# Output projection's second half begun in the score banks, beside the last head's values

## The chip, the cores and the metric

The kernel runs on one core of a Trainium2 chip, as one program. The metric is device time in microseconds (us), the median of several runs. The core's engines are TensorE (PE, its weight loads shown apart as PEld), VectorE (DVE), ScalarE (ACT), GpSimd (POOL) and SyncE (SP, which issues DMAs). Matmuls write to PSUM, which has 8 banks of 512 fp32 columns on 128 partitions; the other engines read it from there.

## The reference

One layer of a streaming encoder: RMSNorm and one input projection, two groups of eight attention heads (latent attention, group A, heads 0 to 7; forgetting attention, group B, heads 8 to 15), one output projection over both groups, and a SwiGLU FFN. It is computed for a new stream of 1040 rows and for 32 rows that continue a cache of 512. Cut to what matters here:

```python
D_MODEL = 1024; D_FF = 2816
mixed = jnp.concatenate([o_a.reshape(B, L, 512), o_b.reshape(B, L, 512)], axis=-1)

def finish_layer(x, mixed, w_out, norm_ffn, w_gate, w_up, w_down):
    x = x + mixed @ w_out
    h = rms_norm(x, norm_ffn)
    return x + (jax.nn.silu(h @ w_gate) * (h @ w_up)) @ w_down

y = rms_norm(x, norm_final)
```

## The kernel before

All 1072 rows (32 and 1040) are columns of transposed tiles. A product in fp32 accuracy is made of three matmuls: each operand is split into a high and a low part (`hi`, `lo`), and hi x hi, hi x lo and lo x hi are added in PSUM. The program has four stages: the projections; attention over heads 8 to 15 and then 0 to 7 (0 to about 689 us with the first stage); the second half of the output projection with the FFN's norm (to about 752); the FFN in 22 blocks of 128 hidden rows and the final norm (to the end).

**Attention.** `attention` walks over the heads. For each it makes the scores (`scores`, into a pair of PSUM banks, tag psS, two pairs), and beside the scores of one set of tiles it steps through the values of the set before (`values`, and after each second head `finish_pair`; the generator `state["pend"]`): transposes into psT, value matmuls into po, ScalarE and VectorE move the results. Between, it steps through a `filler`, other work for TensorE: for heads 0 to 7 this is `out_half`, the output projection's first half (the rows of `w_out` that belong to group B, accumulated in psF, 48 steps, written to DRAM as `sX2`). How often a filler step is taken is `rate`: steps / (25 (heads - 0.7)). At the start of the last head what is left of the filler is drained. After the last head's scores nothing is left to run beside its values and the last `finish_pair`: `for _ in state["pend"]: pass`.

**PSUM.** In attention psS holds 4 banks, psT 2, psO 1 and psF 1. All close with `B.close()`. The stage after opens psG with six single banks and psN with two.

**Output projection, second half.** Eight row blocks m, each with three column chunks (`FC`: 408, 408 and 256 columns), make 24 units. A unit sums k = 0 to 3 with three matmuls each. Units go in groups of four: k = 0, 1, 2 of the four units first, then k = 3 of the four; k = 3 stands for the last pair of heads. VectorE then adds the unit to `x2`, which has been loaded from `sX2`.

**FFN.** For each block f and chunk, `gate_up` makes two products of 24 matmuls (gate, up), which VectorE reads with L877 and L882, and `down` makes, for the block before, eight products of three matmuls, each read by VectorE with L898 (added to `x2`). The weights of the block after are split by ScalarE (`gh`, `dh`) and VectorE (`gl`, `dl`, L68). The last block's third chunk ends in `down_final`, which keeps eight products in four banks.

The order of instructions on each engine is made by a scheduler in the framework from the program and its tiles; each engine then works through its own queue. A tile framework puts the semaphores: an instruction that writes a tile waits for what read or wrote that tile before. Names in the rows are tiles; L12 is line 12.

Of the kernel before, what the change touches and what calls it, by code (L numbers as in the profile page):

```python
# [9 lines left out]
F32 = mybir.dt.float32  # L10
# [39 lines left out]
def trunk(ctx: ExitStack, tc: tile.TileContext, a):  # L50
# [53 lines left out]
    def rows4(t):  # L104
        return t.rearrange("p (k t) -> p k t", k=4)
# [330 lines left out]
    tp = B.enter_context(tc.tile_pool(name="tp", bufs=LAG + 1))  # L436
    st = B.enter_context(tc.tile_pool(name="st", bufs=2))

    psS = B.enter_context(tc.tile_pool(name="psS", bufs=2, space=PSUM))
    psT = B.enter_context(tc.tile_pool(name="psT", bufs=2, space=PSUM))  # L440
    psO = B.enter_context(tc.tile_pool(name="psO", bufs=1, space=PSUM))
    psF = B.enter_context(tc.tile_pool(name="psF", bufs=1, space=PSUM))
# [280 lines left out]
    state = {"pend": iter(()), "n": 0}  # L723

    def attention(hs, filler, steps, last):
        rate, owed = steps / (25.0 * (len(hs) - 0.7)), [0.0]

        def fill():
            if last and h == hs[0] and grps[0][0] == 5:
                return  # L730
            owed[0] += rate
            while owed[0] >= 1:
                next(filler, None)
                owed[0] -= 1

        rs = raw = None
        for h in hs:
            nxt = h + 1 if h + 1 < 16 else 0
            if not (last and h == hs[-1]):
                heads[nxt] = 0  # L740
            ops, v = heads.pop(h)
            if h == hs[-1]:
                for _ in filler:
                    pass
                if not last:
                    masks()
            nops = fetch(nxt) if nxt in heads else None
            if h % 2 == 0:
                rs = st.tile([128, 2, 9], F32, tag="rs", name="rs")
                pool.memset(rs, 1.0)  # L750
                raw = st.tile([128, T], F32, tag="raw", name="raw", bufs=1)
            for grps in (((5, 6, 7, 8),), ((1, 2, 3, 4), (0,))):
                todo = [i for g in grps for i in g]
                P, done = {}, 0
                for j, i in enumerate(todo):
                    P[i] = scores(h, ops, i, rs)
                    fill()
                    while done < (j + 1) * state["n"] // len(todo):
                        next(state["pend"], None)
                        fill()  # L760
                        done += 1
                for _ in state["pend"]:
                    pass
                if nops is not None and len(grps) == 1:
                    heads[nxt] = (nops, fetch_v(nxt))
                gens = [values(h, v, [(i, P[i]) for i in g], raw) for g in grps]
                state["n"] = sum(len(g) + g[0] if g != (0,) else 1 for g in grps)
                if h % 2 == 1 and len(grps) == 2:
                    gens.append(finish_pair(h // 2, rs, raw))
                    state["n"] += 3  # L770
                state["pend"] = chain(*gens)
        for _ in filler:
            pass
# [6 lines left out]
    def masks():  # L780
        B3 = rooms[-1][:106]
        for j, part in enumerate((0, 0, 1)):
            move(B3[32 * j:32 * j + 32], sKR[:, part])
        move(B3[96:106], sMK[0:10])
        mixed["B3"] = B3
# [2 lines left out]
    mixed["A"] = (slot("A_hi"), slot("A_lo"))  # L788

    attention(range(0, 8), out_half(), 48, True)  # L790
    for _ in state["pend"]:
        pass
    B.close()
    hpx.close()
# [2 lines left out]
    with ExitStack() as C:  # L797
# [1 line left out]
        sqp = C.enter_context(tc.tile_pool(name="sqpC", bufs=1, side="right"))  # L799
        ap_ = C.enter_context(tc.tile_pool(name="ap", bufs=2, side="right"))  # L800
        wf = C.enter_context(tc.tile_pool(name="wpf", bufs=2))
        psG = C.enter_context(tc.tile_pool(name="psG", bufs=6, space=PSUM))
        psN = C.enter_context(tc.tile_pool(name="psNF", bufs=2, space=PSUM))

        def ffn_weights(f):
            gh = wf.tile([128, 2, 8, 128], FR, tag="gh", name="gh")
# [23 lines left out]
                marks[1] = eng.tensor_tensor(out=acc[:, cs], in0=acc[:, cs], in1=sq[:, :n], op=ALU.add).ins  # L830

        big = [tuple(rows4(t) for t in mixed[g]) for g in ("A", "B")]
        m_hi, m_lo = big[0]
        W = None
        units = [(m, c) for m in range(8) for c in FC]
        for u0 in range(0, len(units), 4):
            part = []
            for m, (c0, n) in units[u0:u0 + 4]:
                out_weights(8 + m + 2)
                part.append((m, c0, n, psG.tile([128, 512], F32, tag="psG", name="psG"), w_ring[8 + m]))  # L840

            for ks in ((0, 1, 2), (3,)):
                for m, c0, n, ps, w in part:
                    for k in ks:
                        pe.matmul(ps[:, :n], w[0][:, k], m_hi[:, k, c0:c0 + n], start=(k == 0), stop=False)
                        pe.matmul(ps[:, :n], w[0][:, k], m_lo[:, k, c0:c0 + n], start=False, stop=False)
                        pe.matmul(ps[:, :n], w[1][:, k], m_hi[:, k, c0:c0 + n], start=False, stop=(k == 3))
            if u0 == 12:
                W = ffn_weights(0)
            for m, c0, n, ps, w in part:  # L850
                cs = slice(c0, c0 + n)
                dve.tensor_tensor(out=x2[:, m, cs], in0=ps[:, :n], in1=x2[:, m, cs], op=ALU.add)
                square(m, cs, n, dve)
                if m == 7:

                    for k in range(8):
                        hi, lo = (t[:, k % 4, cs] for t in big[k // 4])
                        act.activation(hi, x2[:, k, cs], AF.Copy, scale=g_ffn[:, k:k + 1])
                        dve.scalar_tensor_tensor(lo, x2[:, k, cs], g_ffn[:, k:k + 1], f32(hi), ALU.mult, ALU.subtract)
                    ps = psN.tile([128, 512], F32, tag="psn", name="psn")  # L860
                    pe.matmul(ps[:, :n], ones, acc[:, cs], start=True, stop=True)
                    rsqrt(rb[:, cs], ps, n, D, sqp)


        def gate_up(W, c0, n, ah, al, between=None):
# [1 line left out]
            cs = slice(c0, c0 + n)  # L867

            def product(j):
                ps = psG.tile([128, 512], F32, tag="psG", name="psG")  # L870
                marks[2] = mm3(ps[:, :n], lambda k: gh[:, j, k], lambda k: gl[:, j, k], lambda k: big[k // 4][0][:, k % 4, cs], lambda k: big[k // 4][1][:, k % 4, cs], 8)
                return ps

# [19 lines left out]
        def down(parts, c0, n, norm=False, then=None):  # L893
            cs = slice(c0, c0 + n)
            for m in range(8):
                ps = psG.tile([128, 512], F32, tag="psG", name="psD")
                down_mm(ps[:, :n], m, cs, parts, True, True)
                dve.tensor_tensor(out=x2[:, m, cs], in0=ps[:, :n], in1=x2[:, m, cs], op=ALU.add)  # L898
                if norm:
                    square(m, cs, n, pool if m < 6 else dve)  # L900
                if m == 3 and then is not None:
                    norm_table()
                    final(*then)
# [19 lines left out]
        def down_final(prev, cur, c0, n):  # L923

            cs = slice(c0, c0 + n)
            pairs = [psG.tile([128, 512], F32, tag="psG", name="psD").rearrange("p (a b) -> p a b", a=2) for _ in range(4)]
            for part in (prev, cur):

                with tc.issue_after(marks[2]):
# [159 lines left out]
```

## Time and profile before

| | us |
|---|---|
| median of 3 runs | 1536.96 (1535.45 to 1539.69) |
| the profiled execution | 1537.25 |
| its span | 1535.5 |
| TensorE busy | 1493.0 |
| VectorE busy | 971.5 |
| ScalarE busy | 591.4 |
| mean granted TensorE clock | 0.993 |

The time is read from TensorE: it works all but some 42 us of the span. The page's slices of the span show where it doesn't (in the attention part and at the end), the windows show this per stretch, and the timelines name for an idle time the instruction that ended it. A matmul's row lasts longer than the distance to the next one's start, since they are pipelined; the pitch is read from starts. [...]

### The profile page before, as it was taken

Reading aid. Unit: us, or ns where it says so; the run is one execution under the profiler, and the core shown is the slowest. Engines: PE = TensorE matmul, PEld = TensorE weight load, DVE = VectorE, ACT = ScalarE, POOL = GpSimd, SP = SyncE. Lnnn points to the kernel's source line nnn. Section 1 sums busy time; section 2 is a strip of 40 time slices with the busy share of each in tenths; the row PEclk is TensorE's granted clock in tenths of the full one; section 3 lists DMA queues with packets and bytes.
Section 4 is the critical chain, followed back from the end, with each engine's and each line's share of the span. In section 5 each row is a group of like instructions: output and inputs, shape, how many; then the busy total and the mean of one; then the engine's idle time right before and its main releaser. Section 6 shows DMA issues by size and latency. Waiting matters only on the chain.

```text
span 1535.5 us, 24295 instructions
## 1 busy us (share of the span) xinstructions
PE 1493.0 (97%) x9317; PEld 1433.5 (93%) x9317; DVE 971.5 (63%) x1861; ACT 591.4 (39%) x1198; POOL 198.5 (13%) x331
## 2 busy tenths in 40 slices
PE   9999998999898999989999999999999999999996
PEld 8999997888787898979999999999999999999996
DVE  8874626787966776766855655555555555655547
ACT  7443436777655666654511111111111121111124
POOL 0343242422131211200000000000000000000001
PEclk9999999999999999999999999999999999999999
DMA  6689567778587686515111111111111111111003
GB/s 196 233 258 299 172 210 249 238 218 262 147 238 185 174 212 161 148 41 206 34 50 44 54 42 42 42 42 42 42 42 42 53 58 53 44 42 42 28 1 115
DMA packets 87636, 184.19 MB, mean 120 GB/s; under 512 B 9754, under 2 KB 52954, under 8 KB 87428
## 3 DMA queue, kind: packets, MB, share of 16 engines
q1 hardware_dynamic: 70592, 128.34, 28.8%
q0 software_dynamic: 16928, 54.29, 10.1%
q8 instruction: 74, 1.21, 0.3%
q14 instruction: 42, 0.34, 0.1%
HBM read 123.93 MB, written 58.67 MB: 119 GB/s over the span
## 4 chain that ended last, share of the span: by engine, by line
PE 88%; DVE 4%; ACT 3%; issue 2%; DMA 1%; POOL 1%; DVEq 0%; SPq 0%; POOLq 0%; ACTq 0%
PE psG L122 11%; PE psG L121 11%; PE psG L123 11%; PE psD L890 5%; PE psD L891 5%; PE psD L889 5%; PE psS L589 5%; PE psT L651 4%; PE psA L123 3%; PE psA L121 3%; PE psA L122 3%; PE po L667 2%; PE po L668 2%; PE psA L386 1%; PE psA L387 1%
## 5 line engine op out<-in xcount | busy, mean ns | idle before, releaser
L898 DVE TENSOR_TENSOR x<-psD,x 128x408 f32<-128x408 f32 (+1 forms) x496 | 236.2, 522 | 4.3 <-PE psD L891 4.3
L122 PE MATMUL psG<-B_lo,gh 128*128 128x408 f32 (+1 forms) x528 | 172.8, 327 | 0.0
L121 PE MATMUL psG<-B_hi,gh 128*128 128x408 f32 (+1 forms) x528 | 172.8, 327 | 0.0
L122 PE MATMUL psG<-A_lo,gh 128*128 128x408 f32 (+1 forms) x528 | 172.6, 327 | 0.0
L121 PE MATMUL psG<-A_hi,gh 128*128 128x408 f32 (+1 forms) x528 | 172.3, 326 | 0.0
L891 PE MATMUL psD<-ah,dl 128*128 128x408 f32 (+1 forms) x528 | 172.1, 326 | 0.0
L123 PE MATMUL psG<-B_hi,gl 128*128 128x408 f32 (+1 forms) x528 | 171.8, 325 | 0.0
L123 PE MATMUL psG<-A_hi,gl 128*128 128x408 f32 (+1 forms) x528 | 171.8, 325 | 0.0
L890 PE MATMUL psD<-al,dh 128*128 128x408 f32 (+1 forms) x528 | 171.7, 325 | 0.0
L889 PE MATMUL psD<-ah,dh 128*128 128x408 f32 (+1 forms) x528 | 170.9, 325 | 0.5 <-ACT ah L67 0.5
L878 ACT ACTIVATE sl<-sl 128x408 f32<-128x408 f32 (+1 forms) x66 | 33.1, 503 | 351.3 <-DVE sl L877 351.2
L882 DVE TENSOR_TENSOR sq<-psG,rb 128x408 f32<-128x408 f32 (+1 forms) x66 | 35.0, 530 | 156.5 <-PE psG L123 156.5
L68 DVE TENSOR_TENSOR ptl<-psT,pth 128x512 fp32r<-128x512 f32 x192 | 104.6, 552 | 28.7 <-ACT pth L67 26.6
L592 DVE TENSOR_REDUCE nm<-psS 128x1 f32<-128x656 f32 (+2 forms) x144 | 104.0, 724 | 27.2 <-PE psS L589 25.6
L67 ACT ACTIVATE pth<-psT 128x512 fp32r<-128x512 f32 (+4 forms) x208 | 99.2, 480 | 55.7 <-PE psT L651 46.5
L830 POOL TENSOR_TENSOR acc<-acc,sq 128x408 f32<-128x408 f32 x10 | 10.8, 1076 | 812.4 <-ACT sq L829 811.9
L877 DVE TENSOR_TENSOR sl<-psG,rb 128x408 f32<-128x408 f32 (+1 forms) x66 | 34.9, 530 | 123.0 <-PE psG L123 123.0
L67 ACT ACTIVATE ah<-sl 128x408 fp32r<-128x408 f32 (+1 forms) x66 | 33.2, 503 | 197.2 <-DVE sl L883 125.8
L589 PE MATMUL psS<-b,a 128*128 128x328 f32 (+4 forms) x360 | 99.9, 331 | 7.4 <-ACT pb L597 6.1
L889 PEld LDWEIGHTS psD<-ah,dh 128*128 128x128 f32 x528 | 99.2, 188 | 0.9 <-ACT ah L67 0.7
L122 PEld LDWEIGHTS psG<-B_lo,gh 128*128 128x128 f32 x528 | 99.2, 188 | 0.5 <-issue 0.3
L121 PEld LDWEIGHTS psG<-B_hi,gh 128*128 128x128 f32 x528 | 99.2, 188 | 0.5 <-issue 0.2
(274 smaller groups left out, 3803.5 us busy)
## 6 DMA issues: line engine op xcount, KB each, us to landing
sg<-w_gu SPq DMA_DIRECT2D x44, 512.0 KB
a<-sQ SPq DMA_DIRECT2D x56, 268.0 KB
b<-sK SPq DMA_DIRECT2D x32, 396.0 KB
sg<-w_down SPq DMA_DIRECT2D x22, 512.0 KB
v<-sV SPq DMA_DIRECT2D x16, 512.0 KB
wst<-w_in SPq DMA_DIRECT2D x13, 512.0 KB
sV<-vt POOLq DMA_DIRECT2D x24, 256.0 KB, 4.5
sK<-room POOLq DMA_DIRECT2D x14, 396.0 KB, 4.9
```

The lines of the kernel that those rows point to most:

```text
L67: first = act.activation(hi, src, AF.Copy)
L68: return first.ins, eng.tensor_tensor(out=lo, in0=src, in1=f32(hi), op=ALU.subtract).ins
L121: pe.matmul(ps, whi(k), rhi(k), start=(k == 0), stop=False)
L122: pe.matmul(ps, whi(k), rlo(k), start=False, stop=False)
L123: last = pe.matmul(ps, wlo(k), rhi(k), start=False, stop=(k == K - 1))
L589: pe.matmul(out, qa[:K, t0:t0 + nq], kb[:K, k0 + c:k0 + c + w], start=(j == 0), stop=last)
L592: dve.tensor_reduce(out=nm[:nq, j:j + 1], in_=src, axis=AX.XY if len(src.shape) == 3 else AX.X, op=ALU.max, negate=True)
L651: pe.transpose(out=pt[:, 128 * g:128 * g + 128], in_=tiles[g][1][:, c:c + 128], identity=ident)
L889: pe.matmul(ps, dh[:, m], ah[:, cs], start=first and j == 0, stop=False)
L890: pe.matmul(ps, dh[:, m], al[:, cs], start=False, stop=False)
L891: pe.matmul(ps, dl[:, m], ah[:, cs], start=False, stop=last and j == len(parts) - 1)
L898: dve.tensor_tensor(out=x2[:, m, cs], in0=ps[:, :n], in1=x2[:, m, cs], op=ALU.add)
```

## The change

The pool psS stays open to the end. During the last head the filler isn't drained ahead, and its rate divides by heads - 0.25. Beside the nine steps of the last head's values and `finish_pair`, `begin` draws two psS pairs and fills their four halves with k = 0, 1, 2 of the first four units, one k per step. The first group then has only k = 3 to do. After that six banks go around: the four halves (`early`) and two banks of psG (was six). `bank` deals them out in that order to units, gate/up products and down products alike.

```diff
-    psS = B.enter_context(tc.tile_pool(name="psS", bufs=2, space=PSUM))
+    psS = ctx.enter_context(tc.tile_pool(name="psS", bufs=2, space=PSUM))
...
-        rate, owed = steps / (25.0 * (len(hs) - 0.7)), [0.0]
+        rate, owed = steps / (25.0 * (len(hs) - (0.25 if last else 0.7))), [0.0]
...
-            if h == hs[-1]:
+            if h == hs[-1] and not last:
                 for _ in filler:
                     pass
-                if not last:
-                    masks()
+                masks()
...
+    units = [(m, c) for m in range(8) for c in FC]
+
+    def out_products(unit, ps, ks):
+        (m, (c0, n)), w = unit, w_ring[8 + unit[0]]
+        for k in ks:
+            for j, (wj, t) in enumerate(((0, 0), (0, 1), (1, 0))):
+                pe.matmul(ps[:, :n], w[wj][:, k], rows4(mixed["A"][t])[:, k, c0:c0 + n], start=(k == 0 and j == 0), stop=(k == 3 and j == 2))
+
+    early = []
+
+    def begin():
+        for u in (0, 2):
+            out_weights(10)
+            pair = psS.tile([128, 2, 512], F32, tag="psS", name="psS")
+            for j in range(2):
+                early.append(pair[:, j])
+                for k in range(3):
+                    out_products(units[u + j], pair[:, j], (k,))
+                    yield
+
+    begun = begin()
     for _ in state["pend"]:
+        next(begun, None)
+    for _ in begun:
         pass
     B.close()
...
-        psG = C.enter_context(tc.tile_pool(name="psG", bufs=6, space=PSUM))
+        psG = C.enter_context(tc.tile_pool(name="psG", bufs=2, space=PSUM))
...
+        drawn = [4]
+
+        def bank():
+
+            t = drawn[0] % 6
+            drawn[0] += 1
+            return early[t] if t < 4 else psG.tile([128, 512], F32, tag="psG", name="psG")
...
-                part.append((m, c0, n, psG.tile([128, 512], F32, tag="psG", name="psG"), w_ring[8 + m]))
...
+                part.append((m, c0, n, early[len(part)] if u0 == 0 else bank(), w_ring[8 + m]))
+
+            for ks in ((3,),) if u0 == 0 else ((0, 1, 2), (3,)):
+                for j, (m, c0, n, ps, w) in enumerate(part):
+                    out_products(units[u0 + j], ps, ks)
...
             def product(j):
-                ps = psG.tile([128, 512], F32, tag="psG", name="psG")
+                ps = bank()
...
             for m in range(8):
-                ps = psG.tile([128, 512], F32, tag="psG", name="psD")
+                ps = bank()
...
-            pairs = [psG.tile([128, 512], F32, tag="psG", name="psD").rearrange("p (a b) -> p a b", a=2) for _ in range(4)]
+            pairs = [bank().rearrange("p (a b) -> p a b", a=2) for _ in range(4)]
```

The rows below are queue order, with the tile numbers behind the names and the engines on whose semaphores an instruction waits. In the changed kernel psS_8425 and psS_8513 are the two pairs; a row does not say which half it writes, so the text does. L797, L915 to L917 and L924 of the changed kernel are the lines 845 to 847, 889 to 891 and 898 of before; L903 and L908 are 877 and 882.

On TensorE, at the last head's values, before: the last transposes and values (L706, L637) stand alone, and the projection's first matmul (L845) waits behind them.

```order
L706 MATMUL psT_8488<-ident_62,bc_8474 128x128 x3
L665 MATMUL po_8438<-ptm_2591,v_7937 128x512
L706 MATMUL psT_8500<-ident_62,bc_8482 128x128 [waits DVE_49,Pool_49]
L637 MATMUL po_8502<-pth_8464,v_7937 128x96 [waits DMAHW0_49,DVE_49]
L637 MATMUL po_8502<-pth_8464,v_7937 128x96 x4
L845 MATMUL psG_8558<-A_hi_5600,woh_8066 128x408 [waits DVE_49,PE_49]
```

The same engine in the changed kernel, from the first of the early products (L797) on.

```order
L668 MATMUL po_8285<-ptl_8378,v_7913 128x128
L797 MATMUL psS_8425<-A_hi_5600,woh_8168 128x408
L797 MATMUL psS_8425<-A_lo_5601,woh_8168 128x408
L797 MATMUL psS_8425<-A_hi_5600,wol_8169 128x408
L651 MATMUL psT_8429<-ident_62,pa_8249 128x128 [waits DVE_49]
L651 MATMUL psT_8429<-ident_62,pa_8296 128x128
L651 MATMUL psT_8429<-ident_62,pa_8326 128x128
L665 MATMUL po_8285<-ptm_2591,v_7913 128x512 [waits DMAHW4_49,DMAHW3_49,Pool_49]
L797 MATMUL psS_8425<-A_hi_5600,woh_8168 128x408
```

Three early matmuls each now stand between the steps of the last values.

On TensorE, at the end of an FFN block before: the last two down products of the 256-column chunk, then the next block's first gate/up product (L121). Each takes the next of six banks.

```order
L889 MATMUL psD_11144<-ah_10546,dh_10220 128x256 [waits DVE_49]
L890 MATMUL psD_11144<-al_10547,dh_10220 128x256
L891 MATMUL psD_11144<-ah_10546,dl_10221 128x256
L889 MATMUL psD_11149<-ah_10546,dh_10220 128x256 [waits DVE_49]
L890 MATMUL psD_11149<-al_10547,dh_10220 128x256
L891 MATMUL psD_11149<-ah_10546,dl_10221 128x256
L121 MATMUL psG_11174<-A_hi_5600,gh_10842 128x408 [waits DVE_49]
```

The same place in the changed kernel.

```order
L915 MATMUL psS_8425<-ah_10447,dh_10141 128x256 [waits DVE_49]
L916 MATMUL psS_8425<-al_10448,dh_10141 128x256
L917 MATMUL psS_8425<-ah_10447,dl_10142 128x256
L915 MATMUL psS_8513<-ah_10447,dh_10141 128x256 [waits DVE_49]
L916 MATMUL psS_8513<-al_10448,dh_10141 128x256
L917 MATMUL psS_8513<-ah_10447,dl_10142 128x256
L121 MATMUL psS_8425<-A_hi_5600,gh_10723 128x408 [waits DVE_49]
```

The down products here write the second halves of the two pairs; L121 writes the first half of psS_8425, and the read that its wait names is VectorE's read of the second half, three matmuls back. In the same chunk, ahead of that, between the two gate/up products of the changed kernel:

```order
L123 MATMUL psS_8513<-B_hi_2593,gl_10432 128x256
L915 MATMUL psG_10979<-ah_10447,dh_10141 128x256 [waits Activation_49]
L916 MATMUL psG_10979<-al_10448,dh_10141 128x256
L917 MATMUL psG_10979<-ah_10447,dl_10142 128x256
L915 MATMUL psG_10984<-ah_10447,dh_10141 128x256
L916 MATMUL psG_10984<-al_10448,dh_10141 128x256
L121 MATMUL psS_8513<-A_hi_5600,gh_10431 128x256 [waits DVE_49]
```

L123 ends the first product in one half of psS_8513, L121 begins the second in the other half, five matmuls later; its wait names VectorE's read of the first half (L903). Before, the second product followed the first at once, in another bank.

On VectorE, where the FFN begins, before: the first read of a gate product (L877) follows L110 at once.

```order
L859 SCALAR_TENSOR_TENSOR B_lo_2594<-x2_8541,gains_61,B_hi_2593 128x256 [waits Activation_49]
L110 TENSOR_SCALAR rv_9082<-psn_9080 128x256 [waits DVE_49,PE_49]
L877 TENSOR_TENSOR sl_9108<-psG_9110,rb_8542 128x408
L882 TENSOR_TENSOR sq_9109<-psG_9137,rb_8542 128x408
L114 TENSOR_TENSOR rv_9082<-rv_9082,rr_9084 128x256 [waits DVE_49,Activation_49]
```

In the changed kernel that read is L903.

```order
L110 TENSOR_SCALAR rv_9067<-psn_9065 128x256 [waits DVE_49,PE_49]
L68 TENSOR_TENSOR gl_9076<-sg_9083,gh_9075 128x1024 [waits DMAHW7_49]
L114 TENSOR_TENSOR rv_9067<-rv_9067,rr_9069 128x256 [waits DVE_49,Activation_49]
L68 TENSOR_TENSOR dl_9078<-sg_9087,dh_9077 128x1024 [waits DMAHW0_49]
L115 TENSOR_TENSOR rv_9067<-rv_9067,rr_9069 128x256 [waits DVE_49]
L903 TENSOR_TENSOR sl_9093<-psS_8425,rb_8585 128x408
```

Two weight splits (L68) and two small steps now stand between.

## Rows read from the trace of the kernel before

In the windows the engines' busy times stand in the order PE, PEld, DVE, ACT, POOL, each with its number of instructions. In the timelines the first number is the start, the second how long it took.

**Rows 1.** Page, part 1: engines' busy time, share of span, instructions.

```profile
PE 1493.0 (97%) x9317; PEld 1433.5 (93%) x9317; DVE 971.5 (63%) x1861; ACT 591.4 (39%) x1198; POOL 198.5 (13%) x331
```

**Rows 2.** Windows, last head: stretch, length, engines' busy us, clock, DMA share, GB/s.

```profile
655.00:670.00 15.00, 13.46 (x86) 11.67 (x86) 10.45 (x20) 9.19 (x23) 1.08 (x2) 1.00 0.13 43
...
677.00:685.00 8.00, 6.00 (x40) 4.61 (x38) 5.22 (x11) 4.41 (x10) 1.83 (x6) 1.00 0.01 2
685.00:687.00 2.00, 0.90 (x5) 0.60 (x4) 1.36 (x3) 1.11 (x2) 0.01 (x1) 0.93 0.02 4
687.00:688.80 1.80, 0.71 (x4) 0.57 (x4) 1.54 (x6) 0.83 (x3) 0.00 (x0) 0.50 0.06 19
688.80:693.40 4.60, 4.59 (x14) 4.48 (x15) 0.58 (x2) 0.14 (x1) 0.00 (x0) 0.50 0.98 368
```

**Rows 3.** Timeline, TensorE, last head: start, us, operation, idle before and releaser.

```profile
680.83 0.50 PE L667 MATMUL po<-pth,v 128*128 128x512 f32 x1 [0.42 <-DVE raw L678]
681.16 0.39 PE L668 MATMUL po<-ptl,v 128*128 128x512 f32 x1
681.40 0.34 PE L667 MATMUL po<-pth,v 128*128 128x384 f32 x1
...
686.53 1.18 PE L637 MATMUL po<-pth,v 112*128 112x96 f32 x5 [0.90 <-DVE raw L678]
688.81 0.68 PE L845 MATMUL psG<-A_hi,woh 128*128 128x408 f32 x1 [1.10 <-DVE raw L712]
```

**Rows 4.** Timeline, TensorE's weight loads, last head.

```profile
680.83 0.19 PEld L667 LDWEIGHTS po<-pth,v 128*128 128x128 f32 x1 [0.61 <-DVE raw L678]
```

**Rows 5.** Timeline, VectorE, last head.

```profile
680.09 0.69 DVE L678 TENSOR_TENSOR raw<-po,half 64x512 f32<-64x512 f32 x1
...
688.46 0.20 DVE L712 TENSOR_TENSOR raw<-raw,psT 128x48 f32<-128x48 f32 x1
```

**Rows 6.** Timeline, SyncE's queue, where the projection's second half begins.

```profile
687.74 3.92 SPq L58 DMA_DIRECT2D x<-sX  x8
```

**Rows 7.** Windows, one stretch of the FFN (columns as in Rows 2).

```profile
1004.00:1040.00 36.00, 36.00 (x223) 35.93 (x222) 20.05 (x40) 6.20 (x9) 0.00 (x0) 1.00 0.14 45
```

**Rows 8.** Timeline, TensorE, one FFN block: 256-column chunk, then 408.

```profile
1005.44 0.28 PE L123 MATMUL psG<-B_hi,gl 128*128 128x256 f32 x1
...
1008.29 0.28 PE L123 MATMUL psG<-B_hi,gl 128*128 128x256 f32 x1
...
1011.24 0.35 PE L121 MATMUL psG<-A_hi,gh 128*128 128x408 f32 x1
...
1015.53 0.35 PE L123 MATMUL psG<-B_hi,gl 128*128 128x408 f32 x1
```

**Rows 9.** Timeline, VectorE, same FFN block.

```profile
1005.76 0.42 DVE L877 TENSOR_TENSOR sl<-psG,rb 128x256 f32<-128x256 f32 x1 [1.75 <-PE psG L123]
...
1015.91 0.58 DVE L877 TENSOR_TENSOR sl<-psG,rb 128x408 f32<-128x408 f32 x1 [0.81 <-PE psG L123]
```

**Rows 10.** Timelines at the FFN's start: TensorE, then VectorE.

```profile
738.20 0.36 PE L121 MATMUL psG<-A_hi,gh 128*128 128x408 f32 x1
...
740.05 0.88 PE L861 MATMUL psn<-acc,ones 128*128 128x408 f32 x2
...
740.96 0.35 PE L123 MATMUL psG<-A_hi,gl 128*128 128x408 f32 x1
...
752.55 0.57 DVE L877 TENSOR_TENSOR sl<-psG,rb 128x408 f32<-128x408 f32 x1
...
764.82 2.36 DVE L68 TENSOR_TENSOR gl<-sg,gh 128x1024 fp32r<-128x1024 f32 x2
```

**Rows 11.** Timelines at the end: VectorE, then TensorE.

```profile
1514.06 0.42 DVE L877 TENSOR_TENSOR sl<-psG,rb 128x256 f32<-128x256 f32 x1
...
1512.16 0.29 PE L121 MATMUL psG<-A_hi,gh 128*128 128x256 f32 x1
...
1518.49 0.74 PE L889 MATMUL psD<-ah,dh 128*128 128x256 f32 x4 [0.49 <-ACT ah L67]
```

More of the change, by code (lines that the diff above doesn't have):

```diff
@@ L832, in trunk @@
         big = [tuple(rows4(t) for t in mixed[g]) for g in ("A", "B")]
-        m_hi, m_lo = big[0]
         W = None
-        units = [(m, c) for m in range(8) for c in FC]
         for u0 in range(0, len(units), 4):
@@ L839, in trunk @@
                 out_weights(8 + m + 2)
-                part.append((m, c0, n, psG.tile([128, 512], F32, tag="psG", name="psG"), w_ring[8 + m]))
[L842 to L847, printed above, removed]
+                part.append((m, c0, n, early[len(part)] if u0 == 0 else bank(), w_ring[8 + m]))
+            for ks in ((3,),) if u0 == 0 else ((0, 1, 2), (3,)):
+                for j, (m, c0, n, ps, w) in enumerate(part):
+                    out_products(units[u0 + j], ps, ks)
             if u0 == 12:
```

## The prediction

> **What bounds the kernel now.** I read the page first: TensorE works 97% of the span [rows 1]. So only two things can move the time: gaps on TensorE that go, and gaps that come. The windows around the last head show the gaps that the change aims at [rows 2]. From 677 to 688.8 TensorE works 6.00 + 0.90 + 0.71 = 7.61 of 11.8 us, so 4.2 us are empty; from 655 to 670 another 1.54 are. [...] The FFN, where half of the span goes, has no gap at all: 36.00 of 36.00 us busy [rows 7]. A change that adds waits there pays for each in full.
>
> **The gain at the last head.** The early products are 36 matmuls, 27 of 408 columns and 9 of 256. Their pitch at full clock is (1015.53 - 1011.24) / 23 = 0.187 us and (1008.29 - 1005.44) / 24 = 0.119 us [rows 8], so 6.1 us of work, more than the 4.2 us that are empty beside them. The output projection began at 688.81, behind a VectorE step that ended at 688.66 [rows 3, 5], because its banks were those of the attention pools; score banks that stay need no such end. The clock should not fall any more: 14 matmuls at 4.6 us against 14 x 0.187 = 2.6 gives 2.0 us. The slower rate (48 steps over 7.75 heads and not 7.3, no drain at the last head's start) spreads the first half's products into the 1.54 us. All together at most 4.2 + 2.0 + 1.5 = 7.7 us. Something stays: the last values (L637, 686.53), their sum and the scaling still follow one another on ScalarE and VectorE, and k = 3 of every unit needs their result. From 686.53 to the end of the last step on that chain at 688.66 are 2.1 us [rows 3, 5], for which what is left of the early products is the cover. The loads of x2 (eight from 687.74 on, 0.98 of the DMA share until 693.4 [rows 2, 6]) still start when B's room comes free, and the first evacuations wait for them. I take off 2.2 us and keep **-5.5 us**, with ends -3.5 and -7.7.
>
> **The price in the FFN.** The change takes six single banks and makes them two banks (psG) and two pairs (psS) whose halves are used one by one. In the order of the changed kernel, a matmul that begins a product in one half carries a wait, and the value waited for is VectorE's read of the other half: the dependency is kept by tile, and the tile is the pair. So a pair works as one buffer. In before, the read that a product waits for belongs to a product five products back; now the distances are short at some places. They are counted in matmuls between the last write of the other half and the waiting matmul.
>
> What such a wait needs: from the start of a product's last matmul to VectorE's read 1005.76 - 1005.44 = 0.32 us at 256 columns and 1015.91 - 1015.53 = 0.38 at 408; the read 0.42 and 0.58 [rows 8, 9]; from the end of a read to the matmul that waited 680.83 - (680.09 + 0.69) = 0.05 [rows 3, 5]. Behind such a wait the next matmul comes 0.33 us later, where the next one of that width comes 0.24 later (680.83, 681.16, 681.40), and the row of the weight load starts at 680.83 as well [rows 3, 4]: 0.09 more. In sum 0.32 + 0.42 + 0.05 + 0.09 = 0.88 at 256 columns, 1.10 at 408. What stands between covers 0.119 or 0.187 for each matmul.
>
> At 408 columns the shortest distance is five matmuls, six pitches, 1.12 us: no stall, with a margin near zero. In the 256-column chunk the order has per block: the second gate/up product behind the first one's read, five between, 6 x 0.119 = 0.71, stall 0.17; a down product behind the second one's read, five between, 0.17; and the next block's first product, which takes half 0 of the pair whose half 1 was written last but one, three between, 4 x 0.119 = 0.48, stall 0.40. Two more at distances eight and nine come out near zero if VectorE's queue has no other read ahead; it has (L909 and the split of ah/al stand between the reads), which I put at 0.1 in sum. So 0.17 + 0.17 + 0.40 + 0.1 = 0.85 us per block, and 20 blocks have this pattern: **+17 us**. Lower end: without the 0.09 at each restart 0.08 + 0.08 + 0.31 = 0.47, 9.5 us. Upper end: one of the waits behind a VectorE step of 0.42 more, 1.27 per block, 25 us.
>
> **The price at the FFN's start.** The first block's first product (L903) must be read before product(1) of chunk 0 may start. In before that read starts at 752.55 [rows 10], and four other banks were free meanwhile. In after's queue on VectorE two weight splits and two small steps stand ahead of it: two such splits take 2.36 [rows 10], the small ones 0.42 at most each, together about 3.0, so the read ends at 752.55 + 3.0 + 0.57 = 756.1. TensorE has 48 matmuls of 408 and 48 of 256 before that (14.7 us from 738.20) and the sums of squares, 0.7 for each of three (from 740.05 to 740.96 with one other matmul of 0.19 in it [rows 10]): 738.20 + 14.7 + 1.9 = 754.8. Stall **+1.5 us**, from 0 (the splits taken from earlier places give it back) to 3.3 (the sums covered).
>
> **The price at the end.** The last gate/up's second product takes the other half of the first one's pair, with one matmul between. VectorE's turn for that read comes at 1514.06, behind a queue of scalings, and lasts 0.42 [rows 11], so the product starts at 1514.6 where before it started at 1512.16, 2.4 us late. Its result feeds the down product that began at 1518.49, waiting for ScalarE by 0.49, and the kernel's last chain hangs on that. **+2.3 us**, from 1 (VectorE reaches the read sooner) to 2.8.
>
> **The sum.** -5.5 + 17 + 1.5 + 2.3 = +15.3 us on the profiled execution's own 1537.25 us (span 1535.5 and 1.75 around it), which is 0.3 above the median of 1536.96: 1552.5, and 1552 against the median.
>
> **The rivals.**
> *The weight load is not part of the restart.* Then each short wait costs 0.09 less and the 408-column waits none: 9.5 us in the FFN, 1537.0 - 5.5 + 9.5 + 1.5 + 2.3 = 1544.8, in all 1542 to 1546.5. Against it stands the row at 680.83, where load and matmul start together [rows 3, 4]; that is a 512-column matmul behind a read of `po`, not one of the FFN. [...]
> *VectorE's queue makes the later waits late too.* VectorE's order between the reads holds three steps that no matmul waits for; each that falls before a waited read adds 0.33 to 0.42. With one more per block 1.27 x 20 = 25 us, 1560; with the margins at 408 columns gone too (0.1 us at three places) up to 1566.
> *The shared pairs cost nothing.* That would be so if the matmuls between covered the whole need, that is a need below 0.48 us instead of 0.88. Then only the gain is left: 1537 - 5.5 = 1531.5, faster. The rows of the read alone (0.32 + 0.42 = 0.74) speak against it; it decides at a stall of 0.1 us per block, since 20 x 0.1 + 3.8 = 5.8 would use up the gain.
> *The clock falls in the FFN.* Each short wait empties TensorE for a moment; the only fall to 0.50 in these rows comes after a stretch with more than half empty, and the FFN's stalls would leave 35.5 of 36.3 us of a block busy. If it fell once per block at the 2.0 us of [rows 2], 20 x 2.0 = 40 us more, 1592. [...]
> *The early products do not fill the gap* (the last values still end late and the clock still falls): the gain is 0 to 3.5, 1554 to 1558, inside the forecast's spread.
>
> **How the numbers follow.** Forecast (short waits in the FFN at about 0.85 us per block): 0.66, 1547 to 1559, with 0.04 of it for the gain that does not come. Weight load hidden: 0.13. VectorE's queue: 0.13. Pairs cost nothing: 0.04, and another 0.01 for that with a smaller gain. Clock: 0.03. The predicted time is the forecast's, **1552 us**; the range **1542 to 1565** takes in the second and nearly all of the third. A measurement of this kernel tells 0.3%, 4.6 us, from no change. Faster by more: 0.04. Within: 0.05 (the rest of the free pairs, the lower edge of the hidden weight load, 0.04). Slower: 0.91.
>
> **What would show it.** Right: from one block's first L121 to the next one's 36.3 us, where 144 x 0.187 + 72 x 0.119 = 35.5 stand without a stall (the windows show less of it as idle, since a matmul's row lasts 0.28 us at a pitch of 0.119 [rows 8]); in TensorE's timeline, starts 0.2 to 0.5 us apart, released by VectorE, at the first product of a block and at the second 256-column product, none in the 408-column chunks; TensorE busy from 677 to 690 but for about 2 us, and a granted clock of 1.00 there; the last product(1) starting right behind a read by VectorE. Wrong: FFN blocks as long as before (the waits cost nothing), gaps in the 408-column chunks (need larger than 1.12 us), a clock below 0.99 in the FFN, or a last head as long as before.

## The result and the profile after

| | before | after |
|---|---|---|
| median, us | 1537.24 (1535.45 to 1539.69) | 1560.57 (1559.37 to 1563.25) |
| ratio | | 1.0148 (1.0127 to 1.0170) |
| span of the profiled execution | 1535.5 | 1559.5 |
| TensorE busy | 1493.0 | 1510.6 |
| an FFN block, from its first L121 to the next one's (mean of 19) | 35.37 | 36.33 |

The kernel is 23.3 us slower; 1552 was forecast, with 1542 to 1565 as the range. The span grew by 24.0 us, and milestones of the two TensorE timelines part it: the first gate product starts 3.5 us earlier than before (738.20 and 734.67), the start of the third FFN block is only 0.6 us ahead any more (799.0 and 798.45), 19 blocks later the last block starts 17.7 us behind (1471.11 and 1488.79), and its end is 24.0 behind. So -3.5, then +3.0 at the FFN's start, +18.2 in 19 blocks, +6.3 at the end.

The first line of the page after, which answers to [rows 1]:

```profile
PE 1510.6 (97%) x9317; PEld 1431.3 (92%) x9317; DVE 981.2 (63%) x1861; ACT 590.8 (38%) x1198; POOL 198.7 (13%) x331
```

TensorE's share did not move, and its busy time rose by 17.6 us with the same 9317 matmuls: a matmul's row lasts longer than its pitch (0.28 us against 0.12 at 256 columns, in the rows below), so most of a short wait hides in the rows. The waits are seen at starts. TensorE's timeline after, at the end of an FFN block and between the two 256-column products of the block after it:

```profile
1016.41 0.45 PE L121 MATMUL psS<-A_hi,gh 128*128 128x408 f32 x1 [0.16 <-DVE x L924]
1016.70 0.34 PE L122 MATMUL psS<-A_lo,gh 128*128 128x408 f32 x1
...
1046.83 0.28 PE L916 MATMUL psG<-al,dh 128*128 128x256 f32 x1
1047.04 0.39 PE L121 MATMUL psS<-A_hi,gh 128*128 128x256 f32 x1
1047.26 0.28 PE L122 MATMUL psS<-A_lo,gh 128*128 128x256 f32 x1
...
1052.00 0.28 PE L917 MATMUL psS<-ah,dl 128*128 128x256 f32 x1
1052.12 0.28 PE L915 MATMUL psS<-ah,dh 128*128 128x256 f32 x1
1052.24 0.28 PE L916 MATMUL psS<-al,dh 128*128 128x256 f32 x1
1052.36 0.28 PE L917 MATMUL psS<-ah,dl 128*128 128x256 f32 x1
1052.80 0.46 PE L121 MATMUL psS<-A_hi,gh 128*128 128x408 f32 x1 [0.16 <-DVE x L924]
1053.09 0.35 PE L122 MATMUL psS<-A_lo,gh 128*128 128x408 f32 x1
```

VectorE's timeline of the same places:

```profile
1046.56 0.42 DVE L903 TENSOR_TENSOR sl<-psS,rb 128x256 f32<-128x256 f32 x1 [0.60 <-PE psS L123]
...
1052.32 0.78 DVE L924 TENSOR_TENSOR x<-psS,x 128x256 f32<-128x256 f32 x2
```

Follow the wait at 1052.80, where the next block begins. The product in half 1 of psS_8425 starts its last matmul at 1052.00; VectorE reads it from 1052.32 on, for 0.42 (the first of the two reads in that row); three matmuls into the other pair stand between; L121, which writes half 0, starts at 1052.80, 0.06 after the read's end, and the matmul behind it 0.29 later where 0.19 is the pitch. 0.32 + 0.42 + 0.06 + 0.10 = 0.90 are needed; the sum had 0.88. At 1047.04 the same with five matmuls between: 0.21 and 0.22 from start to start where the pitch is 0.12. A window over one whole block, which answers to [rows 7], still reads almost full:

```profile
1016.41:1052.80 36.39, 36.23 (x217) 35.18 (x217) 20.54 (x40) 6.09 (x10) 0.00 (x0) 1.00 0.15 44
```

The FFN's start, TensorE and then VectorE, which answers to [rows 10]:

```profile
751.18 0.28 PE L123 MATMUL psG<-B_hi,gl 128*128 128x256 f32 x1
753.19 0.45 PE L121 MATMUL psS<-A_hi,gh 128*128 128x408 f32 x1 [1.73 <-DVE sl L903]
...
749.63 1.21 DVE L68 TENSOR_TENSOR gl<-sg,gh 128x1024 fp32r<-128x1024 f32 x1
750.76 0.41 DVE L114 TENSOR_TENSOR rv<-rv,rr 128x256 f32<-128x256 f32 x1
751.09 1.22 DVE L68 TENSOR_TENSOR dl<-sg,dh 128x1024 fp32r<-128x1024 f32 x1
752.23 0.41 DVE L115 TENSOR_TENSOR rv<-rv,rr 128x256 f32<-128x256 f32 x1
752.56 0.57 DVE L903 TENSOR_TENSOR sl<-psS,rb 128x408 f32<-128x408 f32 x1
```

The splits stand where the order had them; the read ends at 753.13 and TensorE, which had its last other matmul at 751.18, waits for it. By starts that is 753.19 - 751.18 - 0.12 + 0.10 behind it = 2.0 us.

The end, TensorE's timeline, then VectorE's ahead of its three longest waits (answers to [rows 11]):

```profile
1517.75 0.35 PE L916 MATMUL psS<-al,dh 128*128 128x408 f32 x1
1518.93 0.46 PE L915 MATMUL psS<-ah,dh 128*128 128x408 f32 x1 [0.83 <-DVE x L924]
...
1526.56 0.28 PE L121 MATMUL psS<-A_hi,gh 128*128 128x256 f32 x1
1527.68 0.45 PE L915 MATMUL psS<-ah,dh 128*128 128x408 f32 x1 [0.84 <-DVE x L924]
...
1530.99 0.95 PE L946 MATMUL psn<-acc,ones 128*128 128x408 f32 x2 [0.28 <-DVE acc L861]
1535.11 0.39 PE L121 MATMUL psS<-A_hi,gh 128*128 128x256 f32 x1 [3.16 <-DVE sl L903]
...
1535.59 0.42 PE L121 MATMUL psS<-A_hi,gh 128*128 128x256 f32 x1
1535.80 0.42 PE L122 MATMUL psS<-A_lo,gh 128*128 128x256 f32 x1
...
1539.57 0.28 PE L915 MATMUL psG<-ah,dh 128*128 128x256 f32 x1
```

```profile
1517.80 0.58 DVE L861 TENSOR_TENSOR acc<-acc,sq 128x408 f32<-128x408 f32 x1 [1.14 <-POOL acc L861]
1518.30 0.58 DVE L924 TENSOR_TENSOR x<-psS,x 128x408 f32<-128x408 f32 x1
...
1526.19 0.95 DVE L116 SCALAR_TENSOR_TENSOR acc<-rv,rr 128x408 f32<-128x408 f32 x1
1527.06 0.57 DVE L924 TENSOR_TENSOR x<-psS,x 128x408 f32<-128x408 f32 x1
...
1532.48 1.74 DVE L938 SCALAR_TENSOR_TENSOR x<-x,gains,acc 128x408 f32<-128x408 f32 x3
1534.14 0.57 DVE L114 TENSOR_TENSOR rv<-rv,rr 128x408 f32<-128x408 f32 x1
1534.64 0.42 DVE L903 TENSOR_TENSOR sl<-psS,rb 128x256 f32<-128x256 f32 x1
```

There are two waits in the last block's down products beside the one at the last gate/up. At 1518.93 TensorE waits for a read that stands in VectorE's queue behind a sum of squares, which itself waited 1.14 us for GpSimd; at 1527.68 for one that stands behind a step of the norm (L116). Then come 3.16 us of idle time before the last gate/up's second product, whose read of the other half (L903, 1534.64) stands behind scalings of the result (L938), and behind that wait a pitch of 0.21 where 0.12 is usual: its 24 matmuls, up to L915 at 1539.57, take 4.46 us and not 24 x 0.119 = 2.86. The windows show why:

```profile
1531.10:1535.10 4.00, 0.85 (x2) 0.19 (x2) 4.00 (x9) 2.38 (x4) 0.00 (x0) 1.00 0.11 42
1535.10:1539.20 4.10, 4.09 (x21) 4.09 (x22) 2.60 (x5) 0.41 (x1) 0.00 (x0) 0.58 0.57 210
```

TensorE worked 0.85 of 4.00 us, and the granted clock of the next 4.1 us is 0.58.

The last head, which answers to [rows 2]:

```profile
677.00:685.00 8.00, 7.89 (x52) 7.26 (x51) 5.58 (x11) 4.65 (x10) 1.96 (x5) 1.00 0.22 69
685.00:687.00 2.00, 2.00 (x18) 1.95 (x17) 0.68 (x1) 0.68 (x2) 0.00 (x0) 1.00 0.00 0
687.00:688.80 1.80, 1.80 (x16) 1.76 (x16) 1.08 (x2) 0.28 (x1) 0.41 (x2) 1.00 0.00 0
688.80:693.40 4.60, 3.92 (x26) 3.41 (x24) 3.07 (x7) 1.96 (x4) 0.00 (x0) 1.00 0.15 22
```

Here the change does what it says: 0.11 us empty where 4.2 were, and the clock stays at 1.00.

### The profile page after: what moved, and what is told of

It reads as the page before. It is cut to its first block, busy times and chain, and to the rows that moved or that the text cites. A ratio compares the mean times of both kernels' runs of the same rounds, so it can differ in the third digit from the quotient of the medians.

```text
span 1559.5 us, 24245 instructions
## 1 busy us (share of the span) xinstructions
PE 1510.6 (97%) x9317; PEld 1431.3 (92%) x9317; DVE 981.2 (63%) x1861; ACT 590.8 (38%) x1198; POOL 198.7 (13%) x331
## 4 chain that ended last, share of the span: by engine, by line
PE 87%; DVE 6%; ACT 3%; issue 2%; DMA 1%; POOL 1%; DVEq 0%; SPq 0%; ACTq 0%; POOLq 0%
PE psS L121 8%; PE psS L122 7%; PE psS L123 7%; PE psS L589 5%; PE psT L651 5%; PE psG L121 4%; PE psS L915 4%; PE psG L123 4%; PE psG L122 4%; PE psS L917 3%; PE psS L916 3%; PE psA L123 3%; PE psA L121 3%; PE psA L122 3%; PE po L667 2%; PE po L668 2%
## 5 line engine op out<-in xcount | busy, mean ns | idle before, releaser
L924 DVE TENSOR_TENSOR x<-psS,x 128x408 f32<-128x408 f32 (+1 forms) x330 | 172.0, 541 | 39.2 <-PE psS L917 38.2
L121 PE MATMUL psS<-A_hi,gh 128*128 128x408 f32 (+1 forms) x360 | 119.4, 332 | 8.2 <-DVE sl L903 4.9
L68 DVE TENSOR_TENSOR ptl<-psT,pth 128x512 fp32r<-128x512 f32 x192 | 104.8, 553 | 31.5 <-ACT pth L67 29.5
L915 PE MATMUL psS<-ah,dh 128*128 128x408 f32 (+1 forms) x348 | 119.8, 344 | 1.7 <-DVE x L924 1.7
L916 PE MATMUL psS<-al,dh 128*128 128x408 f32 (+1 forms) x348 | 115.1, 331 | 0.0
L917 PE MATMUL psS<-ah,dl 128*128 128x408 f32 (+1 forms) x348 | 115.0, 331 | 0.0
L122 PE MATMUL psS<-B_lo,gh 128*128 128x408 f32 (+1 forms) x360 | 114.8, 319 | 0.0
L121 PE MATMUL psS<-B_hi,gh 128*128 128x408 f32 (+1 forms) x360 | 114.5, 318 | 0.0
L122 PE MATMUL psS<-A_lo,gh 128*128 128x408 f32 (+1 forms) x360 | 114.3, 318 | 0.0
L123 PE MATMUL psS<-A_hi,gl 128*128 128x408 f32 (+1 forms) x360 | 114.2, 317 | 0.0
L123 PE MATMUL psS<-B_hi,gl 128*128 128x408 f32 (+1 forms) x360 | 113.9, 317 | 0.0
L908 DVE TENSOR_TENSOR sq<-psS,rb 128x408 f32<-128x408 f32 (+1 forms) x45 | 22.9, 509 | 114.4 <-PE psS L123 114.4
L121 PEld LDWEIGHTS psS<-A_hi,gh 128*128 128x128 f32 x360 | 67.9, 188 | 19.5 <-DVE x L924 7.3
L924 DVE TENSOR_TENSOR x<-psG,x 128x408 f32<-128x408 f32 (+1 forms) x166 | 79.5, 499 | 1.0 <-PE psG L917 1.0
```

What stands on the lines that cost most here:

```text
L68: return first.ins, eng.tensor_tensor(out=lo, in0=src, in1=f32(hi), op=ALU.subtract).ins
L121: pe.matmul(ps, whi(k), rhi(k), start=(k == 0), stop=False)
L122: pe.matmul(ps, whi(k), rlo(k), start=False, stop=False)
L123: last = pe.matmul(ps, wlo(k), rhi(k), start=False, stop=(k == K - 1))
L915: pe.matmul(ps, dh[:, m], ah[:, cs], start=first and j == 0, stop=False)
L916: pe.matmul(ps, dh[:, m], al[:, cs], start=False, stop=False)
```

## The experiments

Each ratio is against the kernel before in the same set of runs. The **theory** was: the dependency is kept by pair, so the short distance between its halves costs 0.96 us per FFN block and most of the end; the early start itself is a gain. The main **rival**: the FFN is longer because the early start makes the scheduler set it in another order, or because the clock falls.

**The early start with six single banks.** The score pairs are given back after the first group, and four single banks take their place.

```diff
-    psS = ctx.enter_context(tc.tile_pool(name="psS", bufs=2, space=PSUM))
+    S = ctx.enter_context(ExitStack())
+    psS = S.enter_context(tc.tile_pool(name="psS", bufs=2, space=PSUM, side="right"))
...
-        drawn = [4]
+        drawn, psH = [0], []
...
-            return early[t] if t < 4 else psG.tile(...)
+            return (psG if t < 2 else psH[0]).tile(...)
...
+            if u0 == 0:
+                S.close()
+                psH.append(C.enter_context(tc.tile_pool(name="psH", bufs=4, space=PSUM, side="right")))
```

> The early start as in the changed kernel, but the two score pairs are given back once the first group of four units has been read, and four single banks take their place, so that six single banks go around in the rest as before. Theory (the dependency kept by pair makes the FFN's blocks 0.96 us longer, and the end): FFN blocks of 35.4 us as before, and what is left is the gain of the early start, which stood 6.4 us ahead in the changed kernel's trace between 490 and 735 us: 1531 us, 1529 to 1534. Rival (the blocks are longer because the output projection starts elsewhere and the scheduler sets the FFN in another order, or because the clock falls): over 1550.

Measured: 1532.42 us, ratio 0.9962 (0.9947 to 0.9977). An FFN block takes 35.37 us again. The theory holds: the early start stays, and with singles the loss is gone. The order of work changes with it, too: each chunk of a block is again 48 gate/up matmuls and then 24 down matmuls, as before, where the changed kernel's queue mixes them (five down matmuls between two gate/up products, for one). The next run shows whether the pairs or the early start bring that order. This window answers to [rows 7]:

```profile
1004.00:1040.00 36.00, 36.00 (x224) 35.93 (x223) 20.67 (x42) 6.62 (x10) 0.00 (x0) 1.00 0.14 45
```

**The pairs alone.** The kernel before, with two singles and the halves of two pairs in place of six singles.

```diff
-        psG = C.enter_context(tc.tile_pool(name="psG", bufs=6, space=PSUM))
+        psG = C.enter_context(tc.tile_pool(name="psG", bufs=2, space=PSUM))
+        psP = C.enter_context(tc.tile_pool(name="psP", bufs=2, space=PSUM))
+        early, drawn = [], [0]
+        for _ in range(2):
+            pair = psP.tile([128, 2, 512], F32, tag="psP", name="psP")
+            early += [pair[:, 0], pair[:, 1]]
...
+            return early[t] if t < 4 else psG.tile(...)
```

> The kernel before, with no early start and with its pacing, but the six single banks of the second half are two single banks and the four halves of two pairs, dealt out as in the changed kernel. Theory: the price of the pairs alone: 20 blocks at 0.96 us, 2 to 3 us at the FFN's start and some 5 us at the end more: 1537 + 19 + 3 + 5 = 1564, 1559 to 1568. Rival (pairs alone cost little; it is the early start that costs): 1537 to 1545.

Measured: 1561.25 us, ratio 1.0152 (1.0136 to 1.0169), blocks of 36.34 us. The price is there without the early start, and a block has the changed kernel's order of work: the pairs bring both, so this part of the rival falls. The order by itself costs nothing that can be seen: counted over 19 blocks of the changed kernel, nine of a block's 216 matmuls start more than 0.025 us behind the pitch, 0.98 us in sum, and the others keep it; before, none is late. The clock's part falls too: from 734.67 to 1488.79 the changed kernel's granted clock is 1.00. The run also showed something not looked for. TensorE's timeline:

```profile
679.77 0.45 PE L856 MATMUL psG<-A_hi,woh 128*128 128x408 f32 x1 [0.47 <-ACT pa L597]
...
684.83 0.33 PE L856 MATMUL psG<-A_hi,woh 128*128 128x256 f32 x1
```

L856 is the projection's second half. Nothing in this kernel puts it there by hand, and before it began at 688.81 [rows 3]: the smaller pool psG let the scheduler move two units up, the first from 679.77 on, the second from 684.83 (an expectation below takes 684.8 for the first). The FFN's first product starts at 735.05, 3.2 us earlier than before, so the pairs' own price is the 23.1 us that the span grew by and these 3.2, some 26 us.

**The halves apart.** The changed kernel, with the banks dealt out so that the halves of a pair are three products apart.

```diff
-        drawn = [4]
+        drawn = [0]
...
-            t = drawn[0] % 6
+            t = (4, 0, 2, 5, 1, 3)[drawn[0] % 6]
```

> The changed kernel, but the six banks go around in an order in which the two halves of a pair are three products apart (single, half 0 of pair 1, half 0 of pair 2, single, half 1 of pair 1, half 1 of pair 2). Theory: the waits stay, their distances grow: in the 256-column chunk the order has five, six and seven matmuls between where it had three, five and five, which leaves about 0.2 to 0.3 us per block: 5 us, and about 3 at the end: 1531 + 8 = 1539, 1535 to 1544. Rival (it is the count of waits or the kind of bank, not the distance): blocks of 36.3 us as in the changed kernel, 1555 to 1562.

Measured: 1539.81 us, ratio 1.0013 (1.0004 to 1.0023). The kernel has the same pairs, and waits of the same kind, and 21 us less. It is the distance that counts: five matmuls of a block are late now, 0.42 us in sum, where nine were, 0.98. (The scheduler's order is another one again.) A block takes 35.76 us, 0.39 more than with singles, where the changed kernel has 0.96; 20 x 0.57 = 11.4 us come back there, and most of the rest at the FFN's start and the end.

**The old pacing.** The changed kernel with the filler's rate and drain of before.

```diff
-        rate, owed = steps / (25.0 * (len(hs) - (0.25 if last else 0.7))), [0.0]
+        rate, owed = steps / (25.0 * (len(hs) - 0.7)), [0.0]
...
-            if h == hs[-1] and not last:
+            if h == hs[-1]:
```

> The changed kernel with the filler's pacing of before: the rate over heads - 0.7, and the rest of the filler drained at the last head's start. Theory: most of the gain comes from the early products beside the last values and from the clock that does not fall at 687 us, not from the pacing, so the time is 0 to 2 us longer than the changed kernel's 1560.6: 1560.6 to 1562.6. Rival (the pacing brings the gain): 1564 to 1567. Should the pacing itself cost (the changed kernel's clock fell once more, at 470 us, where only the pacing is different): 1558.

Measured: 1560.68 us, ratio 1.0146 (1.0131 to 1.0162), against 1.0148 of the changed kernel. Pacing is worth nothing that can be told here, and costs nothing; both rivals fall.

**The pool split, nothing else.** From what the pairs alone had shown: the kernel before, with its pool of six split into four and two.

```diff
-        psG = C.enter_context(tc.tile_pool(name="psG", bufs=6, space=PSUM))
+        psG = C.enter_context(tc.tile_pool(name="psG", bufs=4, space=PSUM))
+        psH = C.enter_context(tc.tile_pool(name="psH", bufs=2, space=PSUM))
...
+            t = drawn[0] % 6
+            return (psG if t < 4 else psH).tile(...)
```

> The kernel before with one edit: the pool of six single banks of the second half is split into one of four (where the score pairs lay) and one of two, dealt out in turn. No early start is written, the pacing is that of before. Theory (what held the first products back to 688.8 us was that the pool of six lay over all of the attention's PSUM pools and so waited for the last of them; in the run with pairs alone the products into the two banks of a smaller pool began at 684.8 us by themselves): the scheduler moves the first units ahead by itself, the FFN keeps its six singles, and the time is near that of the early start with six singles, 1532.4: 1531 to 1535. Rival (the early start has to be written beside the values, or the four banks only come free with the last scores' reads): 1536.5 to 1539.

Measured: 1532.51 us, ratio 0.9957 (0.9943 to 0.9971): the whole gain of the early start, with no early start written. TensorE's timeline (L853 to L855 are the projection's products, L637 the last values):

```profile
679.99 0.46 PE L853 MATMUL psG<-A_hi,woh 128*128 128x408 f32 x1 [0.47 <-ACT pa L597]
...
688.71 0.66 PE L637 MATMUL po<-pth,v 112*128 112x96 f32 x5
689.20 0.35 PE L853 MATMUL psG<-A_hi,woh 128*128 128x256 f32 x1
```

The first product starts 8.8 us earlier than in [rows 3], behind the last read of the scores (L597). So what held it in the kernel before is shown: not the order of the program but the pool of six. It lay over more than the four score banks: in [rows 3] its first matmul waits for L712, which reads psT [rows 5].

**The split pool with the new pacing.**

```diff
-        rate, owed = steps / (25.0 * (len(hs) - 0.7)), [0.0]
+        rate, owed = steps / (25.0 * (len(hs) - (0.25 if last else 0.7))), [0.0]
...
-            if h == hs[-1]:
+            if h == hs[-1] and not last:
```

> The same split of the pool, and the changed kernel's pacing of the filler (48 steps over 7.75 heads, no drain at the last head's start). Theory (pacing is worth nothing by itself, as the changed kernel with the old pacing showed): within 1.5 us of the split pool alone, 1531 to 1535. Rival (pacing fills the gaps of 655 to 670 us, and so gains where no pair costs): 1.5 to 3 us less than the split pool alone.

Measured: 1531.61 us, ratio 0.9952 (0.9935 to 0.9969). It is the lowest median of all, but not to be told from the split alone.

**A single bank at the end.** The changed kernel, with one bank skipped before the last gate/up's second product.

```diff
             if between is not None:
                 between()
+                drawn[0] += 1
             ps = product(1)
```

> The changed kernel, but the last gate/up's second product takes a bank of psG and not the other half of the first product's pair. Theory: of the 6.3 us that the end lost, 2.6 are the wait for VectorE's read of the other half and 2.15 the half clock that followed that wait; both go, the two waits of 1.1 us in the last block's down products stay: 1560.6 - 4.75 = 1555.8, 1554.5 to 1557.5. Rival (VectorE's queue of scalings sets the end anyway): 1559 to 1561. Second rival (the wait goes but the clock falls for another reason): 1558.

Measured: 1557.72 us, ratio 1.0118 (1.0100 to 1.0136), 0.30% under the changed kernel's ratio, with intervals that overlap, and 0.2 us above the range expected. What it is worth is read from the traces: there the stretch from the last block's start to the end takes 67.65 us, against 70.71 of the changed kernel and 64.39 before. So 3.1 of the 6.3 us go, not 4.75 (the two parts, put at 2.6 and 2.15 in the expectation, are 3.2 and 1.6 by the rows shown above; the sum stays). The wait and the low clock are gone (the granted clock is 1.00 from 1510 to 1540 us), but TensorE then waits elsewhere, 1.69 us:

```profile
1538.06 0.28 PE L918 MATMUL psS<-ah,dl 128*128 128x256 f32 x1
1540.02 0.39 PE L916 MATMUL psG<-ah,dh 128*128 128x256 f32 x1 [1.69 <-ACT ah L67]
```

VectorE, ahead of it:

```profile
1537.47 1.19 DVE L939 SCALAR_TENSOR_TENSOR x<-x,gains,acc 128x408 f32<-128x408 f32 x2
1538.58 0.41 DVE L909 TENSOR_TENSOR sq<-psG,rb 128x256 f32<-128x256 f32 x1
```

`ah` comes from ScalarE, behind VectorE's queue of scalings (L939) and the read of the second product (L909), as in [rows 11] where it cost 0.49. So the rival, that this queue sets the end, holds in part. The two waits in the down products stay (0.84 us of idle time each). The expectation counted the whole 4.8 us as path; 1.7 of them had covered this wait, and 4.8 - 1.7 comes to the 3.1 measured.

## Why the prediction was right, and where it was off

The direction and the mechanism were right: the pairs alone cost 1.5% (net of 3.2 us that the scheduler's own early start saves there), and without them the early start gains 0.4%. The changed kernel lies some 28 us above the early start with six singles, and the prices read from the traces, 19.2 in the FFN's blocks, 2.0 at its start and 6.3 at the end, make 27.5.

- **The gain, -5.5.** Six singles with the early start gave 1532.42 against 1538.21, -5.8 us. In the changed kernel's own trace only 3.5 are seen, because it stood 2.9 us behind at 481 us (at the same score matmul of both traces); from there on it wins 6.4. Its clock was low for longer around there: in 466 to 490 us the mean granted clock is 0.79 and 0.93 before, with 99 matmuls and 116. Of the change only the filler's rate is meant to reach that stretch, and two kernels with the same rate (six singles, and the bank skipped at the end) read 0.93, so the rate is not shown as the cause. The step that set the clock's fall at 687 us down as removed (2.0 us, from the 14 matmuls at 0.50 in [rows 2]) held: from 685 to 690 us the granted clock is 1.00 in the changed kernel, with six singles, with the pairs alone and with the split pool, where TensorE works 4.1 to 5.0 of those 5.0 us.
- **The FFN, +17.** 0.96 us per block and 20 blocks make 19.2; the sum had 0.85. Its parts are in the rows: 0.32 and 0.10 at the block's first product (0.40 forecast), 0.09 + 0.10 at the second product and again at the down product behind it (0.17 each). The rest of 0.16 (0.1 forecast for VectorE's queue) are starts late by less than 0.1, partly in the 408-column chunks, for which a margin near zero had been found (the matmul behind the one at 1028.82 comes 0.06 late).
- **The rivals in the FFN.** The restart costs what the sum had: behind the wait at 1047.04 the next matmul comes 0.10 us late (0.09 forecast), where the rival of the hidden weight load had it on time. In the stream a load's row starts one pitch ahead of its own matmul (1046.72, for the matmul at 1046.83); behind the wait it starts with it (1047.04), as at 680.83 before. That the load is what makes the next matmul late is the author's reading of these rows; no run shows it apart.

```profile
1046.72 0.19 PEld L916 LDWEIGHTS psG<-al,dh 128*128 128x128 f32 x1
1047.04 0.19 PEld L121 LDWEIGHTS psS<-A_hi,gh 128*128 128x128 f32 x1
```

  The clock did not fall in the FFN (1.00 from 734.67 to 1488.79), with waits of 0.2 to 0.44 us from start to start in every block. VectorE's queue did not delay the reads behind the three larger waits of a block: they start 0.32 us after the last matmul. It did delay some others, at the price of the small late starts: the bank written at 1028.82 had its last matmul at 1026.96, and VectorE read it only from 1028.15 on, behind L924 and L909.
- **The FFN's start, +1.5.** 2.0 measured, by the mechanism forecast. Its working was loose by some tenths: three times 0.7 is 2.1 and not 1.9, and 756.1 - 754.8 is 1.3 before the restart is added. Both ends of the wait came some 3 us earlier than worked out, since the working used the times of before without the gain.
- **The end, +2.3.** This is the term that failed in size: 6.3. The wait for the last gate/up's first read is there (3.2 us, 2.4 forecast). What the step left out: two waits of about 1 us in the last block's down products, where VectorE's queue holds steps of the norm, one of which waits for GpSimd; and the lower clock behind the long wait, 4.46 us instead of 2.86. That is 2.0 + 3.2 + 1.6, and 0.2 for the restarts behind the first two: 7.0. Against it stand two waits of before: the one for `ah` of [rows 11], 0.65 by starts, is gone, and the one for the norm's sum, 0.81 in the row below, has 0.28 left (at 1530.99). 7.0 - 0.65 - 0.5 makes 5.8 of the 6.3; the other 0.5, in starts late by 0.1 or less, stays open. The forecast had walked the FFN's regular blocks by distance and turned to the last block for one wait only. TensorE before:

```profile
1510.42 0.95 PE L920 MATMUL psn<-acc,ones 128*128 128x408 f32 x2 [0.81 <-DVE acc L830]
```

- **The sum.** 0.5 + 2.2 + 4.0 more than forecast in the three prices make 6.7, and 22 us would follow from -5.5; measured are 23.3. The range up to 1565 had room for the miss. That room had been made for VectorE's queue inside the blocks; the end, where most of the miss arose, had been given 2.8 at most, so that the time fell inside is in part luck.

## What to carry to other kernels

A tile that is used in halves is one buffer for whatever tracks dependencies by tile: before a pair takes the place of two singles, count the work between the last write of one half and the first of the other, and compare it with read latency + read + restart (here 0.32 + 0.42 + 0.06 + 0.10 = 0.90 us for a read of 256 columns). A pool that lies over several old pools waits for the last of them (here its first matmul came at 688.81 us, and at 679.99 with the pool split); splitting it by what lay below can bring the overlap that a change tries to write by hand. In a kernel where one engine has no gap, walk the irregular last iteration wait by wait: other work stands in the readers' queue there (here 3.16 us of idle time at one wait).

## What the runs showed of the hardware

In the changed kernel, a matmul that has waited for a read by VectorE starts 0.05 to 0.06 us after the read's end (0.05 at 1518.93, 0.06 at 1047.04), and at a granted clock of 1.00 the matmul behind it comes 0.10 us late, at 256 columns (0.22 from start to start, pitch 0.12) and at 408 (0.29, pitch 0.19); the weight load's row starts with the matmul that waited (1047.04). Waits of this kind, some three per block of 36.33 us, left the granted clock at 1.00 (734.67 to 1488.79); behind a stretch near the end with 0.85 of 4.00 us worked it was 0.58 on average over 4.1 us. Where attention passes from one group of heads to the other, at 466 to 490 us, the clock fell in every run's profile, but for different lengths (mean granted clock 0.79 to 0.93 over nine kernels whose work there is nearly the same), and the changed kernel, with 0.79, lost 2.4 us there on the kernel before between 424 and 481 us. Each profile holds one execution; the cause stays open.
